# Latent attention's query columns: multiplied by pairs of heads, the rotated ones by fours

## The chip, the cores and the metric

One core of a Trainium2 chip runs the whole program: TensorE (PE) multiplies into PSUM banks, VectorE (DVE) and ScalarE (ACT) read these banks and write SBUF, GpSimd (POOL) works from SBUF to SBUF, SyncE (SP) issues the loads of weights. The metric is the device time of one launch in microseconds.

## The reference, cut to what matters

Two layers over 256 latent and 256 context tokens (512 in layer 0; in layer 1 queries are made for 256 tokens only). One of three branches of a layer is a latent attention with 8 heads. Its query vector has 64 plain and 32 rotated elements per head:

```
q = to_heads(rmsnorm(pq, lp['mla_q_norm_g']) @ lp['mla_w_uq'], MLA_HEADS)
q_nope, q_rope = q[..., :MLA_NOPE], q[..., MLA_NOPE:]
q_rope = apply_rope(q_rope, *rope)        # the 256 latent tokens only
q = jnp.concatenate([q_nope, q_rope], axis=-1)
s = jnp.einsum('bhqd,bhkd->bhqk', qi, k).astype(f32) * scale
```

`mla_w_uq` has 256 rows and 8 x 96 = 768 columns; head h owns columns 96h to 96h + 95, the last 32 of them rotated.

## The kernel before

Everything is float32 in effect: an operand is embedded in a float32r high part and a remainder (`split2`: ACT makes the high part, another engine subtracts), and `mm3` multiplies high by high, low by high and high by low, on lines 279, 280 and 281. A product over 256 rows is thus six multiplications.

`mla(l, nt)` has a stage ahead (projections, norms; `qn` the normed query input, `cn` the normed key/value input, both split) and a main stage. `split_uq` splits the query weights `raw` into `wqh` and `wql` in one piece of 128 x 1536. The main stage goes over four pairs of heads. `prod(p)` makes a pair's operands: one group of three multiplications for the keys of both heads, copied to `kh` and `kl`; then for each head six multiplications with 96 columns of weights into one PSUM bank of tag `g`; `rope` (L797 to L800) on rows 64 to 95 of that bank, four DVE operations on 32 x 256; and `split_scaled` (L803 on ACT, L804 on DVE) of all 96 rows into the head's tiles `qh` and `ql`. `A(h, u)` multiplies scores out of `qh`, `ql`, `kh`, `kl` into a bank of tag `s`: query blocks 0 and 1 against all 512 keys, in layer 0 also the context block. Maximum, exponential, transposes (`B`) and the product with the values (`C`) follow, two steps later.

Tag `g` has two banks. They serve keys, queries and also the convolution branch's and the gates' products that are woven in between. `qh` and `ql` have three tiles each. Temporaries come from a ring `t` of nine tiles (`t2k`). Steps are written as lists that are woven together and put in order by a table; each engine's instruction order then comes from the scheduler of the framework when the program is built, so that a change in one place moves neighbours on other engines. In layer 0 the multiplications of the modulation vectors (L347) stand between as work that waits for nothing here. POOL has only remainders (L219) and casts (L231) of weights, and a few convolution operations, in this stage.

`pick(key, default)` looks up which engine does a small copy.

Of the kernel before, what the change touches and what calls it, by code (L numbers as in the profile page):

```python
# [10 lines left out]
F32R = mybir.dt.float32r  # L11
# [7 lines left out]
D = 1024  # L19
# [3 lines left out]
MLA_SCALE = 96.0 ** -0.5  # L23
# [101 lines left out]
def backbone_kernel(ctx: ExitStack, tc: tile.TileContext, t, out):  # L125
# [3 lines left out]
    KDUP, WLO = "ee", (nc.vector, nc.vector)  # L129
# [5 lines left out]
    PE, ACT, DVE, POOL, SP = nc.tensor, nc.scalar, nc.vector, nc.gpsimd, nc.sync  # L135
# [25 lines left out]
    def t2k(dt=F32):  # L161
        return tmp.tile([128, 512], dt, tag="t", name="t")

    def bank(tag, bufs=2):
        return psum.tile([128, 512], F32, tag=tag, name=tag, bufs=bufs)
# [34 lines left out]
    def pick(key, default):  # L200
        return CHOICE.get(key, default)
# [4 lines left out]
    def cp(key, default="A"):  # L206

        return {"A": ACT.copy, "D": DVE.tensor_copy, "P": POOL.tensor_copy}[pick(key, default)]
# [66 lines left out]
    def mm3(ps, pairs, first=True, last=True):  # L275

        n = len(pairs)
        for i, (ah, al, bh, bl) in enumerate(pairs):
            PE.matmul(ps, lhsT=ah, rhs=bh, start=first and i == 0, stop=False)  # L279
            PE.matmul(ps, lhsT=ah, rhs=bl, start=False, stop=False)  # L280
            PE.matmul(ps, lhsT=al, rhs=bh, start=False, stop=last and i == n - 1)  # L281

    def split2(hi, lo, src, eng=DVE):

        ACT.copy(hi, src)
        eng.tensor_tensor(out=lo, in0=src, in1=hi.bitcast(F32), op=ALU.subtract)
# [506 lines left out]
    def rope(ps, rows, scr=True):  # L793

        a, b = t2k(), t2k()
        v = ps[rows, 0:NL]
        DVE.tensor_tensor(out=a[rows, 0:NL], in0=v, in1=rs[rows, :], op=ALU.mult)  # L797
        DVE.tensor_tensor(out=v, in0=v, in1=rc[rows, :], op=ALU.mult)
        DVE.stream_shuffle(out=b[rows, 0:NL], in_=a[rows, 0:NL], mask=SWAP16)
        DVE.tensor_tensor(out=v, in0=v, in1=b[rows, 0:NL], op=ALU.add)  # L800

    def split_scaled(hi, lo, src, scale):
        ACT.activation(out=hi, in_=src, func=AF.Copy, scale=scale)  # L803
        DVE.scalar_tensor_tensor(out=lo, in0=src, scalar=scale, in1=hi.bitcast(F32), op0=ALU.mult, op1=ALU.subtract)  # L804
# [58 lines left out]
    def mla(l, nt):  # L863

        pre, main = [], []
        box = {}
# [91 lines left out]

        def split_uq(raw, u):
            m = S["mla"]  # L960
            box["wq"] = (m.tile([128, 2, 768], F32R, name="wqh"), m.tile([128, 2, 768], F32R, name="wql"))
            split2(box["wq"][0], box["wq"][1], raw, WLO[l])

        bu = Blk(load_uq)
        bv = Blk(load_ukv)
        pre.append(Step(lambda u: None, Unit(bu, split_uq, late=True)))
        pre.append(Step(g_v, Unit(bv, split_ukv, late=True)))

        qt = {}

        def prod(p):
            def f():
                m = S["mla"]
                ps = bank("g")
                kc = slice(2 * p, 2 * p + 2)
                mm3(ps, [(box["wk"][0][:, kc, :].rearrange("p h d -> p (h d)"),
                          box["wk"][1][:, kc, :].rearrange("p h d -> p (h d)"), box["cn"][0], box["cn"][1])])
                for i in range(2):
                    kb = box["k"][(2 * p + i) % 3]
                    cp(f"kh{l}.{2 * p + i}")(kb[0][0:64, :], ps[64 * i:64 * i + 64, :])  # L980
                    DVE.tensor_tensor(out=kb[1][0:64, :], in0=ps[64 * i:64 * i + 64, :], in1=kb[0][0:64, :].bitcast(F32), op=ALU.subtract)
                for i in range(2):
                    h = 2 * p + i
                    ps = bank("g")
                    wc = slice(96 * h, 96 * h + 96)
                    mm3(ps[0:96, :nt], [(box["wq"][0][:, k, wc], box["wq"][1][:, k, wc],
                                         box["qn"][0][:, k, :], box["qn"][1][:, k, :]) for k in range(2)])
                    rope(ps, slice(64, 96))
                    qh = m.tile([128, nt], F32R, tag="qh", name="qh", bufs=3)
                    ql = m.tile([128, nt], F32R, tag="ql", name="ql", bufs=3)  # L990
                    split_scaled(qh[0:96, :], ql[0:96, :], ps[0:96, :nt], MLA_SCALE)
                    qt[h] = (qh, ql)
            return Step(f)

# [40 lines left out]
        for n in range(len(seq) + LAG + 2):  # L1035
            if n < len(seq):
                p, u, i = seq[n]
# [3 lines left out]
            if 0 <= n - LAG < len(seq):  # L1041
                p, u, i = seq[n - LAG]
# [641 lines left out]
```

## Time and profile before

| | us |
|---|---|
| three runs, median (lowest, highest) | 1326.32 (1324.16, 1326.61) |
| the profiled execution | 1327.46 |
| its span, first to last instruction | 1325.7 |
| PE busy | 1281.5 (97%) |
| DVE, ACT, POOL busy | 868.3 (66%), 579.7 (44%), 262.9 (20%) |

The span is what lies between the first and the last instruction; the execution's own time has 1.8 us more around it. Sums are made against that one execution. The two main stages that the change touches lie at about 97 to 195 us (layer 0) and 915 to 970 us (layer 1).

### The profile page before, as it was taken

How to read it: one execution, taken by the hardware profiler on the slowest of the kernel's cores; microseconds unless marked ns; L12 is line 12 of the kernel's file. 1: busy time of each engine (PE TensorE's matmuls, PEld its weight loads, DVE VectorE, ACT ScalarE, POOL GpSimd, SP SyncE). 2: the span in 40 equal slices, each digit the busy share in tenths (PEclk: the TensorE clock that was granted, in tenths of full speed). 3: DMA queues.
4: the chain of work that ended last, by engine and by line, in shares of the span. 5: the costliest groups of instructions: out<-in, count | busy, mean ns of one | idle time of the engine just before them, and what ended most of it. 6: DMA issues, size and time to landing. Idle time of an engine off the chain costs nothing. (4 is left out here: it accounts for less than half of the span.)

```text
span 1325.7 us, 19880 instructions
## 1 busy us (share of the span) xinstructions
PE 1281.5 (97%) x7934; PEld 1077.5 (81%) x7934; DVE 868.3 (66%) x1426; ACT 579.7 (44%) x1027; POOL 262.9 (20%) x233
## 2 busy tenths in 40 slices
PE   5999999999999999999999999998999999999997
PEld 3566777678888798787787877996788999999997
DVE  4776746865243568987584875588768557876555
ACT  4454552664222334332432331364546755645343
POOL 3111032210002112220100112122133343240210
PEclk8899999999999999999999999998999999999999
DMA  9643234443332324655563543332124355555552
GB/s 283 166 160 106 77 123 133 149 138 95 95 96 95 120 72 130 220 178 167 177 207 114 185 153 123 120 104 80 49 81 124 120 175 187 159 188 189 174 183 94
DMA packets 159790, 185.21 MB, mean 140 GB/s; under 512 B 4880, under 2 KB 149233, under 8 KB 157650
## 3 DMA queue, kind: packets, MB, share of 16 engines
q1 hardware_dynamic: 158162, 182.27, 43.7%
q0 software_dynamic: 928, 1.54, 0.4%
q8 instruction: 62, 1.02, 0.3%
q14 instruction: 30, 0.25, 0.1%
q10 hardware_dynamic: 608, 0.14, 0.0%
HBM read 182.88 MB, written 1.05 MB: 139 GB/s over the span
## 5 line engine op out<-in xcount | busy, mean ns | idle before, releaser
L231 ACT CAST whi<-raw 128x1024 fp32r<-128x1024 f32 x197 | 206.7, 1051 | 429.8 <-PE g L280 201.5
L279 PE MATMUL g<-hhi,whi 128*128 128x512 f32 (+2 forms) x1040 | 354.3, 341 | 4.3 <-DVE d L1179 1.7
L281 PE MATMUL g<-hhi,wlo 128*128 128x512 f32 (+2 forms) x1040 | 352.3, 339 | 0.1
L280 PE MATMUL g<-hlo,whi 128*128 128x512 f32 (+2 forms) x1040 | 351.9, 339 | 0.5 <-DVE hlo L506 0.5
L219 POOL TENSOR_TENSOR wlo<-raw,whi 128x512 fp32r<-128x512 f32 x138 | 187.6, 1380 | 647.3 <-ACT whi L231 508.2
L219 DVE TENSOR_TENSOR wlo<-raw,whi 128x1024 fp32r<-128x1024 f32 x161 | 199.7, 1242 | 151.0 <-ACT whi L231 144.5
L279 PEld LDWEIGHTS g<-hhi,whi 128*128 128x128 f32 x1040 | 195.4, 188 | 36.2 <-issue 4.7
L280 PEld LDWEIGHTS g<-hlo,whi 128*128 128x128 f32 x1040 | 196.1, 189 | 23.5 <-DVE hlo L506 0.7
L281 PEld LDWEIGHTS g<-hhi,wlo 128*128 128x128 f32 x1040 | 196.0, 189 | 22.7 <-issue 0.3
L383 DVE SCALAR_TENSOR_TENSOR macc<-modr,spad,macc 128x1024 f32<-128x1024 f32 x84 | 111.9, 1364 | 8.2 <-DMA modr<-in_w_mod_dram 7.5
L1364 DVE SCALAR_TENSOR_TENSOR x<-s,modT,x 128x256 f32<-128x256 f32 x95 | 43.5, 480 | 72.0 <-PE s L281 72.0
L281 PE MATMUL s<-hid0h,wlo 128*128 128x512 f32 (+1 forms) x256 | 86.9, 339 | 0.0
L280 PE MATMUL s<-hid0l,whi 128*128 128x512 f32 (+1 forms) x256 | 86.8, 339 | 0.0
L279 PE MATMUL s<-hid0h,whi 128*128 128x512 f32 (+1 forms) x256 | 86.7, 339 | 0.0
L279 PE MATMUL s<-hid1h,whi 128*128 128x256 f32 (+1 forms) x224 | 72.8, 325 | 0.0
L281 PE MATMUL s<-hid1h,wlo 128*128 128x256 f32 (+1 forms) x224 | 72.4, 323 | 0.0
L280 PE MATMUL s<-hid1l,whi 128*128 128x256 f32 (+1 forms) x224 | 72.4, 323 | 0.0
L809 DVE TENSOR_REDUCE sm<-s 128x1 f32<-128x512 f32 (+1 forms) x75 | 51.1, 689 | 30.2 <-PE s L281 17.3
L279 PEld LDWEIGHTS s<-hid0h,whi 128*128 128x128 f32 x256 | 48.4, 189 | 8.2 <-issue 1.7
L281 PEld LDWEIGHTS s<-hid0h,wlo 128*128 128x128 f32 x256 | 48.1, 188 | 5.7
L280 PEld LDWEIGHTS s<-hid0l,whi 128*128 128x128 f32 x256 | 48.0, 187 | 5.8
L157 ACT ACTIVATE t<-s,sm 128x512 f32<-128x512 f32 (+1 forms) x67 | 40.8, 614 | 26.0 <-DVE sm L809 25.7
(470 smaller groups left out, 2414.2 us busy)
## 6 DMA issues: line engine op xcount, KB each, us to landing
raw<-in_w_fc_dram SPq DMA_DIRECT2D x64, 1024.0 KB, 5.4
raw<-in_w_in_dram SPq DMA_DIRECT2D x34, 1024.0 KB, 5.3
modr<-in_w_mod_dram SPq DMA_DIRECT2D x48, 512.0 KB, 4.1
raw<-in_w_mod_dram SPq DMA_DIRECT2D x16, 1024.0 KB, 5.0
mq<-in_w_mod_dram SPq DMA_DIRECT2D x16, 512.0 KB, 7.7
raw<-in_w_out_dram SPq DMA_DIRECT2D x8, 1024.0 KB, 5.1
raw<-in_w_in_dram SPq DMA_DIRECT2D x8, 512.0 KB, 3.8
raw<-in_w_br_a_dram SPq DMA_DIRECT2D x8, 512.0 KB, 3.5
```

The lines of the kernel that those rows point to most:

```text
L157: ins = ACT.activation(out=out, in_=in_, func=func, **kw).ins
L219: e.tensor_tensor(out=u.lo[:, a:a + w], in0=src[:, a:a + w], in1=u.hi[:, a:a + w].bitcast(F32), op=ALU.subtract)
L231: cp(f"hi{u.id}")(u.hi, src)
L279: PE.matmul(ps, lhsT=ah, rhs=bh, start=first and i == 0, stop=False)
L280: PE.matmul(ps, lhsT=ah, rhs=bl, start=False, stop=False)
L281: PE.matmul(ps, lhsT=al, rhs=bh, start=False, stop=last and i == n - 1)
L383: DVE.scalar_tensor_tensor(out=a, in0=raw, scalar=sv, in1=a, op0=ALU.mult, op1=ALU.add)
L809: DVE.tensor_reduce(out=sm[:, c0:c0 + nseg], in_=ps.rearrange("p (s k) -> p s k", s=nseg), axis=AX.X, op=ALU.max, negate=True)
L1364: DVE.scalar_tensor_tensor(out=x[:, n, c], in0=ps[:, c], scalar=modT[l][:, goff + n, s:s + 1], in1=x[:, n, c], op0=ALU.mult, op1=ALU.add)
```

## The change

`split_uq` writes the columns in a new order: first the 64 plain columns of all heads (0 to 511), then the 32 rotated columns of all heads (512 to 767). It does so in four pieces (plain and rotated, for each of the two row halves). `prod(p)` multiplies the plain columns of both heads at once, 128 columns. In pairs 0 and 2 a further group multiplies the rotated columns of the next four heads, also 128; these are rotated together on 128 rows, scaled and split together into two tiles of the ring `t`, kept in `box["qr"]` for this pair and the next. Each head's `qh` and `ql` then get 64 rows from the pair's bank and 32 rows by a copy out of the common tiles, on POOL, since no key `qr...` is in the table of choices.

```diff
@@ -958,8 +958,13 @@
 
         def split_uq(raw, u):
             m = S["mla"]
+
             box["wq"] = (m.tile([128, 2, 768], F32R, name="wqh"), m.tile([128, 2, 768], F32R, name="wql"))
-            split2(box["wq"][0], box["wq"][1], raw, WLO[l])
+            for c0, d0, d in ((0, 0, 64), (512, 64, 32)):
+                hi, lo = [w[:, :, c0:c0 + 8 * d].rearrange("p k (h d) -> p k h d", d=d) for w in box["wq"]]
+                src = raw.rearrange("p k (h d) -> p k h d", d=96)[:, :, :, d0:d0 + d]
+                for k in range(2):
+                    split2(hi[:, k], lo[:, k], src[:, k], WLO[l])
 
         bu = Blk(load_uq)
         bv = Blk(load_ukv)
@@ -979,16 +984,27 @@
                     kb = box["k"][(2 * p + i) % 3]
                     cp(f"kh{l}.{2 * p + i}")(kb[0][0:64, :], ps[64 * i:64 * i + 64, :])
                     DVE.tensor_tensor(out=kb[1][0:64, :], in0=ps[64 * i:64 * i + 64, :], in1=kb[0][0:64, :].bitcast(F32), op=ALU.subtract)
+                def q_cols(c0):
+                    ps = bank("g")
+                    wc = slice(c0, c0 + 128)
+                    mm3(ps[:, :nt], [(box["wq"][0][:, k, wc], box["wq"][1][:, k, wc],
+                                      box["qn"][0][:, k, :], box["qn"][1][:, k, :]) for k in range(2)])
+                    return ps
+                if p % 2 == 0:
+                    ps = q_cols(512 + 64 * p)
+                    rope(ps, slice(0, 128))
+                    box["qr"] = (t2k(F32R)[:, :nt], t2k(F32R)[:, :nt])
+                    split_scaled(box["qr"][0], box["qr"][1], ps[:, :nt], MLA_SCALE)
+                ps = q_cols(128 * p)
                 for i in range(2):
                     h = 2 * p + i
-                    ps = bank("g")
-                    wc = slice(96 * h, 96 * h + 96)
-                    mm3(ps[0:96, :nt], [(box["wq"][0][:, k, wc], box["wq"][1][:, k, wc],
-                                         box["qn"][0][:, k, :], box["qn"][1][:, k, :]) for k in range(2)])
-                    rope(ps, slice(64, 96))
                     qh = m.tile([128, nt], F32R, tag="qh", name="qh", bufs=3)
                     ql = m.tile([128, nt], F32R, tag="ql", name="ql", bufs=3)
-                    split_scaled(qh[0:96, :], ql[0:96, :], ps[0:96, :nt], MLA_SCALE)
+                    split_scaled(qh[0:64, :], ql[0:64, :], ps[64 * i:64 * i + 64, :nt], MLA_SCALE)
+                    rows = slice(32 * (h % 4), 32 * (h % 4) + 32)
+                    for j, dst in enumerate((qh, ql)):
+                        e = pick(f"qr{l}.{h}.{j}", "P")
+                        {"P": POOL.tensor_copy, "D": DVE.tensor_copy, "A": ACT.copy}[e](dst[64:96, :], box["qr"][j][rows, :])
                     qt[h] = (qh, ql)
             return Step(f)
```

POOL in layer 0, from the weights' remainder ahead of pair 0 to the one after pair 1, before (`wlo` and `whi` are parts of weights, a number behind a name tells one tile from another):

```order
L483 TENSOR_TENSOR hlo_179<-t_433,hhi_178 128x256
L219 TENSOR_TENSOR wlo_863<-raw_850,whi_862 128x512 x2
L219 TENSOR_TENSOR wlo_1106<-raw_850,whi_1105 128x512 x2
L231 CAST whi_1546<-raw_1444 128x1024
L219 TENSOR_TENSOR wlo_1547<-raw_1444,whi_1546 128x512 x2
L219 TENSOR_TENSOR wlo_1552<-raw_1444,whi_1551 128x512 x2
```

and now, where `t_915` and `t_916` are the common high and low tile of heads 0 to 3:

```order
L219 TENSOR_TENSOR wlo_1099<-raw_856,whi_1098 128x512 x2
L1007 COPY qh_926<-t_915 32x512
L1007 COPY qh_932<-t_915 32x512
L1007 COPY ql_927<-t_916 32x512
L1007 COPY ql_933<-t_916 32x512
L1007 COPY qh_1038<-t_915 32x512
L1007 COPY ql_1039<-t_916 32x512
L231 CAST whi_1526<-raw_1439 128x1024
L219 TENSOR_TENSOR wlo_1527<-raw_1439,whi_1526 128x512 x2
L1007 COPY qh_1044<-t_915 32x512
L1007 COPY ql_1045<-t_916 32x512
L219 TENSOR_TENSOR wlo_1532<-raw_1439,whi_1531 128x512 x2
```

The copies stand in POOL's queue as high, high, low, low for heads 0 and 1; those of head 3 (`qh_1044`, `ql_1045`) have come behind a cast and a remainder.

TensorE in layer 0, pair 2, around the second group of query columns, before (`g_1252` is the bank of head 5, `s_1285` scores of head 4):

```order
L850 MATMUL o_1269<-t_1213,vtok_867 64x128
L347 MATMUL mod_1309<-raw_1544,spad_91 32x512 x3
L347 MATMUL mod_1309<-raw_1556,spad_91 32x512
L279 MATMUL s_1285<-kh1_772,qh_1248 128x512
L279 MATMUL g_1252<-qnh_706,wqh_846 96x512
L280 MATMUL g_1252<-qnl_707,wqh_846 96x512
L281 MATMUL g_1252<-qnh_706,wql_847 96x512
L279 MATMUL g_1252<-qnh_706,wqh_846 96x512
L280 MATMUL g_1252<-qnl_707,wqh_846 96x512
```

and now, where `g_1245` is the bank of the pair's plain columns (`t_1343` is a bank for transposes):

```order
L850 MATMUL o_1264<-t_1206,vtok_873 64x128
L347 MATMUL mod_1304<-raw_1524,spad_91 32x512 x2
L837 MATMUL t_1343<-ident_73,t_1215 128x128 x2
L279 MATMUL g_1245<-qnh_706,wqh_846 128x512
L280 MATMUL g_1245<-qnl_707,wqh_846 128x512
L281 MATMUL g_1245<-qnh_706,wql_847 128x512
L279 MATMUL g_1245<-qnh_706,wqh_846 128x512
L280 MATMUL g_1245<-qnl_707,wqh_846 128x512
L281 MATMUL g_1245<-qnh_706,wql_847 128x512
```

The scores of head 4 have gone behind the group, and two of the rows of L347 have gone from ahead of it.

ACT in layer 1, pair 2, before (`qh_7850` is head 4's tile, out of its own bank `g_7837`):

```order
L980 CAST kh1_7410<-g_7829 64x512
L157 ACTIVATE t_7825,ss_7739<-s_7821,sm_7826 128x512
L980 CAST kh2_7412<-g_7829 64x512
L803 ACTIVATE qh_7850<-g_7837 96x256
L840 COPY t_7876<-t_7871 128x512
L157 ACTIVATE t_7882,ss_7884<-s_7878,sm_7883 128x512
L803 ACTIVATE qh_7867<-g_7854 96x256
```

and now, where `g_7827` holds the plain columns of heads 4 and 5, and `t_7823` is the common high tile of heads 4 to 7:

```order
L985 CAST kh1_7390<-g_7802 64x512
L157 ACTIVATE t_7798,ss_7712<-s_7794,sm_7799 128x512
L985 CAST kh2_7392<-g_7802 64x512
L803 ACTIVATE qh_7834<-g_7827 64x256
L803 ACTIVATE t_7823<-g_7810 128x256
L840 COPY t_7851<-t_7846 128x512
L803 ACTIVATE qh_7840<-g_7827 64x256
L157 ACTIVATE t_7857,ss_7859<-s_7853,sm_7858 128x512
```

Head 4's plain rows are taken ahead of the common rotated tile, from a bank whose group comes later on TensorE.

## Rows read from the trace of the kernel before

**Rows 1.** Page, part 1: busy time, share of the span, instructions of each engine.

```profile
PE 1281.5 (97%) x7934; PEld 1077.5 (81%) x7934; DVE 868.3 (66%) x1426; ACT 579.7 (44%) x1027; POOL 262.9 (20%) x233
```

**Rows 2.** TensorE's waits, 205 to 1325 us: waiter, ender, sum, times, longest.

```profile
PE g L279 <- DVE x L1079: 2.6, 2, 2.5
...
PE g L279 <- ACT ge L1308: 0.2, 1, 0.2
```

**Rows 3.** Tile wqh, whole run: count, min/median/max ns, first and last start.

```profile
L279 PE MATMUL g<-qnh,wqh x32: 278/390/480, 97.6 to 954.3; 128*96 128x512 f32 x16, 128*96 128x256 f32 x16
...
L286 DVE TENSOR_TENSOR wql<-raw,wqh x2: 1748/1757/1766, 74.7 to 883.3; 128x1536 fp32r<-128x1536 f32 x2
```

**Rows 4.** Timeline, TensorE, layer 0, 512 tokens: start, length, line, tiles.

```profile
97.36 0.39 PE L281 MATMUL g<-cnh,wkl 128*128 128x512 f32 x1
97.59 0.39 PE L279 MATMUL g<-qnh,wqh 128*96 128x512 f32 x1
97.82 0.39 PE L280 MATMUL g<-qnl,wqh 128*96 128x512 f32 x1
```

**Rows 5.** Timeline, TensorE, layer 1, 256 tokens.

```profile
936.99 0.28 PE L279 MATMUL g<-qnh,wqh 128*96 128x256 f32 x1
937.11 0.28 PE L280 MATMUL g<-qnl,wqh 128*96 128x256 f32 x1
...
942.50 0.28 PE L279 MATMUL g<-hhi,whi 128*128 128x256 f32 x1
942.62 0.28 PE L280 MATMUL g<-hlo,whi 128*128 128x256 f32 x1
```

**Rows 6.** Line 1182 (copies of 32 rows), and timelines of POOL and DVE.

```profile
L1182 POOL CAST d<-d x21: 389/610/1629, 197.4 to 1017.0; 32x512 fp32r<-32x512 f32 x18, 32x256 fp32r<-32x256 f32 x3
...
1014.35 1.63 POOL L1182 CAST d<-d 32x512 fp32r<-32x512 f32 x1 [1.35 <-ACT d L1178]
...
1014.29 1.22 DVE L219 TENSOR_TENSOR wlo<-raw,whi 128x1024 fp32r<-128x1024 f32 x1
...
111.62 1.03 POOL L231 CAST whi<-raw 128x1024 fp32r<-128x1024 f32 x1 [16.42 <-PE s L281]
```

**Rows 7.** Timeline, layer 0, heads 0 and 1, DVE and TensorE.

```profile
102.38 0.69 DVE L804 SCALAR_TENSOR_TENSOR ql<-g,qh 96x512 fp32r<-96x512 f32 x1 [0.71 <-ACT qh L803]
...
103.95 0.39 PE L281 MATMUL s<-kh,ql 96*128 96x512 f32 x1
...
106.37 0.33 PE L837 MATMUL t<-ident,t 128*128 128x128 f32 x1 [0.33 <-ACT t L157]
106.85 0.50 PE L279 MATMUL s<-kh,qh 96*128 96x512 f32 x1 [0.15 <-ACT qh L803]
```

**Rows 8.** Timeline, layer 0, pair 2, TensorE and DVE.

```profile
137.97 1.07 PE L347 MATMUL mod<-raw,spad 128*32 128x512 f32 x8
...
139.31 0.40 PE L279 MATMUL g<-qnh,wqh 128*96 128x512 f32 x1
...
138.39 0.69 DVE L804 SCALAR_TENSOR_TENSOR ql<-g,qh 96x512 fp32r<-96x512 f32 x1
```

**Rows 9.** Layer 1: a window's busy times and granted clock, then timeline rows.

```profile
core 0: us, PE busy (x) PEld busy (x) DVE busy (x) ACT busy (x) POOL busy (x), PEclk, DMA share, GB/s
917.00:924.00 7.00, 5.66 (x17) 4.25 (x16) 5.57 (x15) 1.65 (x5) 0.00 (x0) 0.51 0.00 0
...
918.92 0.80 PE L279 MATMUL s<-kh,qh 96*128 96x512 f32 x1 [1.34 <-ACT qh L803]
...
920.37 0.63 PE L279 MATMUL g<-cnh,wkh 128*128 128x512 f32 x1
920.80 0.63 PE L280 MATMUL g<-cnl,wkh 128*128 128x512 f32 x1
...
940.16 0.33 PE L279 MATMUL g<-qnh,wqh 128*96 128x256 f32 x1 [0.25 <-DVE kl L981]
...
941.70 0.50 PE L279 MATMUL s<-kh,qh 96*128 96x512 f32 x1 [0.61 <-ACT qh L803]
...
941.26 0.38 ACT L803 ACTIVATE qh<-g 96x256 fp32r<-96x256 f32 x1 [2.16 <-DVE g L800]
```

## The prediction

> **What bounds the kernel now.** I read the page's first part, then TensorE's waits, then the two stages that the change touches as a timeline. The first row to see is that TensorE is busy for 97% of the span [rows 1]. That alone says little, since a busy engine may still be waiting for its next operand, so the second view is what ended its idle time after 205 us: the list has 19 rows, the largest is 2.6 us, the smallest 0.2, every one names a compute engine and none a DMA [rows 2]. Two things follow. A multiplication that is no longer there shortens the run by its distance from the next one, wherever TensorE's queue is dense. And time won early is kept: no transfer is waited for later that would take it back.
>
> **The multiplications.** One head's query columns are six multiplications with 96 columns of weights; in both layers together that is 32 on each of the three lines, so 96 [rows 3]. After the change one pair takes six with 128 columns, and every second pair six more for the rotated columns of four heads: per layer (4 + 2) x 6 = 36 in place of 48. The price of one is the distance to the next start. With 512 tokens (layer 0) it is 0.23 us behind 128 columns of weights and 0.23 behind 96 [rows 4]; with 256 tokens (layer 1) 0.12 behind either [rows 5]. So the wider weights cost nothing and the 24 that go are worth 12 x 0.23 + 12 x 0.12 = 4.2 us. All of them go in the odd pairs: pair 1 and pair 3 have six where they had twelve, while pairs 0 and 2 keep twelve.
>
> **What the change adds to the way from the multiplication to the scores.** Before: rotation on DVE, scaled copy on ACT, remainder on DVE, then the scores. Now a head's scores also need its 32 rotated rows copied by POOL from the common tile, one copy for the high part and one for the low. Such copies are in the trace elsewhere: 0.61 us for 512 columns, 0.39 for 256, once 1.63 [rows 6]. I follow the four places where the queues could not hide them.
>
> Layer 0, pair 0. The first scores start as before, since the rotation group stands where head 0's group stood. The remainder of that group ended at 102.38 + 0.69 = 103.07 and the scores' third multiplication, which reads it, began at 103.95 [rows 7]. In POOL's new order two high copies are in front of the low one, but they need only ACT's part and run while DVE makes the remainder; the low copy begins at about 103.6 and ends at 104.2. That is 0.25 us late, and the new order of TensorE puts one key multiplication ahead of it: between 0 and 0.25, taken 0.15. On the other side head 1 no longer has a rotation of its own: the idle of 0.33 at 106.37 and of 0.15 at 106.85 [rows 7] closes, and with it one slower first multiplication, 0.6 together. Bounds of this place: -0.75 to +0.5 (if copies in a row leave gaps), taken -0.45.
>
> Layer 0, pair 2. The pair's group needs the bank that the rotation group holds until DVE has taken the remainder. Before, the second group began at 139.31, and from 137.97 on eight modulation multiplications (1.07 us) and one of the scores stood in front of it [rows 8]. In the new order half of the eight stand there and the one of the scores comes later, so on the old scale TensorE would be there at 137.97 + 0.5 = 138.5, while DVE's remainder ends at 138.39 + 0.69 = 139.1. So 0.6 us are laid bare, 0.7 with a slower first multiplication; none if DVE, with fewer operations, comes that much earlier. Taken 0.7, ends 0 and 1.5.
>
> Layer 1, pair 0. Here everything waits already: TensorE runs at half clock from 917 to 924, granted 0.51 [rows 9]. The copies replace the second rotation that DVE put between; taken +0.15, ends 0 and 0.6.
>
> Layer 1, pair 2. Scores began at 941.70, 0.44 after ACT began its scaled copy of 0.38, at 941.26, with 0.61 us idle [rows 9]. Now ACT takes head 4's plain rows first; these wait for the pair's group, which begins at 940.16; its last of six starts 0.64 later and takes 0.28 [rows 5]. So about 941.1, plus 0.38 for these, 0.38 for the rotated tile, 0.4 for POOL's copy: 942.3. That is 0.6 more, and the low copy comes fourth in POOL's queue (0.39 each), 0.25 more after what TensorE has to fill with. Taken +0.85, ends 0.4 and 1.5. Before pair 3 DVE makes no rotation any more, so a wait like the 0.25 us at 940.16 (for a key remainder that stands behind a rotation [rows 9]) goes there: -0.2.
>
> **Off the path.** The rotation: eight times four operations become two times four per layer, on four times the rows; DVE gets time back, but where TensorE waits for it is counted above, so nothing more. The weights' split was one remainder of 1.76 us [rows 3]; in four pieces, each at most as long as the remainder of 0.69 in [rows 8], it is 2.8 at most. It lies at 74.7 and 883.3 us, over twenty us ahead of its use; nothing. In layer 1 the scheduler places some of its surroundings anew, among conv operations that TensorE waits for (up to 2.6 us by [rows 2]); I see neither sign, 0 with ends -0.7 and +0.7. The transfers of the transform tables, which POOL issues behind the copies, are wanted only after the stage.
>
> **The sum**, against the profiled execution: -4.2 (multiplications) - 0.45 + 0.7 (layer 0) + 0.15 + 0.85 - 0.2 (layer 1) = -3.15 us. Its time is 1327.46 us (span 1325.7, 1.8 around it), so 1324.3; the median of the runs shown, 1326.32, lies 1.1 below that execution, so as a median I say 1323.2. With every place at its upper end (0.5, 1.5, 0.6, 1.5, and 0.7 ahead of layer 1's stage) nothing is left, +0.4; with every one at its lower end (-0.75, 0, 0, 0.4, -0.7) it is -5.5.
>
> **Rivals.**
> *The chains eat it.* POOL's copies are behind one another and, in layer 0, head 3's two stand behind a cast and a remainder of weights. That cast began at 111.62 after a wait of 16.42 us for TensorE [rows 6]; cast, remainder and copies are done some 5 us later, at 117, and head 3's scores come at about 119. If the places come out half way to their upper ends, 1.8 of the 3.15 goes: 1325.0. For it: all four are chains over three engines, which I read from one execution. Against: the idle in the trace where such chains stand is small.
> *The clock.* The low stretch from 917 costs 0.20 us for each multiplication of 512 columns (distance 0.43 in [rows 9] against 0.23), eleven of them, and 0.10 for two of 256: 2.4. It came after idle of 2.5 [rows 2] and 1.34 us [rows 9] on TensorE. If the shorter rotation of pair 0 (one in place of two on DVE) or other work there keeps the clock up: 1323.2 - 2.4 = 1320.8. If instead the idle at layer 1's pair 2 (0.25 and 0.61 before, some 1.5 then) brings a second such stretch: 1325.6.
> *Copies at the long price (the slower side).* One copy of the 21 took 1.63 us in place of 0.61; it began at 1014.35, beside a DVE subtraction of 1.22 at 1014.29 whose two inputs both lie in SBUF [rows 6]. If the copies here met the same, each on the path would cost 1.0 in layer 0 and 0.65 in layer 1; three and two of them stand in a row in front of scores in layer 0 (pairs 0 and 2), five and four in layer 1: 5 x 1.0 + 9 x 0.65 = 10.9 us, so 1323.2 + 10.9 = 1334. It decides from six long copies on: these eat the 3.15 and 2.65 more. Against it: beside the copies DVE mostly has one input in PSUM here (rotation, remainders, maxima); its subtractions of two SBUF tiles come once per pair, for the outputs.
> This is where a rule speaks against the change. The Trainium skill, "SBUF — State Buffer", section "Who interferes with whom", says: "A DVE instruction with two SBUF inputs contends with a GpSimd instruction that reads SBUF", and that the first to issue holds the shared port for its whole length. The copy of 1.63 us agrees with it; by that rule taken for every copy the time is the 1334 above, and by the row of 0.61, which the other copies show, it is the forecast.
> *It does not do what it says* would be 24 multiplications still there; the order of the new program excludes it.
>
> **How the numbers follow.** A measurement of this kernel tells about 0.2% from no change, so 2.65 us, and the forecast lies just beyond. Chances: forecast 0.52 (1321.8 to 1324.8; 0.34 of it past 2.65, 0.18 short of it); the clock kept up or layer 1's start better placed 0.12, faster; the chains 0.22, within 0.2%; a second low stretch 0.04, within; long copies or a queue that POOL blocks 0.10, slower. Faster 0.46, same 0.44, slower 0.10. The range takes in all but the last and the outermost ends: 1319.8 to 1327.0.
>
> **What would show it.** In the new profile TensorE must have 24 multiplications fewer, still 0.23 and 0.12 apart. At 104 us the scores' low part comes some 0.2 later, and the idle at 106.4 is gone. At about 137 us idle of 0.5 to 0.9 ends with DVE's remainder of the rotated tile. At about 940 us the idle in front of the scores is over 1 us and ends with POOL. The copies take 0.61 and 0.39. If pair 1 of layer 0 doesn't end two microseconds earlier than before, the first step is wrong; if the clock is low elsewhere than near 917 to 924, or copies of over 1 us stand in front of scores, a rival holds; if DMA waits appear on TensorE after 205 us, the claim that time is kept is wrong.

## The result: slower, 1.0064 of the time before

| | us |
|---|---|
| before, median of 4 runs beside the changed kernel's (lowest, highest) | 1326.46 (1324.16, 1326.81) |
| after, median of 4 runs (lowest, highest) | 1334.12 (1331.61, 1337.11) |
| ratio of after to before, 95% interval | 1.0064 (1.0050 to 1.0078) |
| profiled execution of after, its span | 1331.61, 1329.6 |

The prediction was 1323.2 within 1319.8 to 1327.0. The measured time is 10.9 above the forecast and 7.1 above the range. The first part of the page of after answers to [rows 1]:

```profile
PE 1281.5 (96%) x7910; PEld 1077.3 (81%) x7910; DVE 850.9 (64%) x1376; ACT 582.6 (44%) x1037; POOL 279.8 (21%) x265
```

TensorE has the promised 24 instructions fewer, and yet it is busy just as long: 1281.5 us. Fewer instructions and no less busy time means that something else on TensorE became dearer. The pitch did not: behind 128 columns of weights it is 0.23 us in layer 0 and 0.12 in layer 1, as said. The timeline of after, TensorE, one stretch of each layer (start, length, line, tiles):

```profile
95.70 0.40 PE L279 MATMUL g<-qnh,wqh 128*128 128x512 f32 x1
95.94 0.39 PE L280 MATMUL g<-qnl,wqh 128*128 128x512 f32 x1
...
939.79 0.28 PE L280 MATMUL g<-qnl,wqh 128*128 128x256 f32 x1
939.90 0.28 PE L281 MATMUL g<-qnh,wql 128*128 128x256 f32 x1
```

### Where the time went

To find the place I matched each multiplication of the two traces by its line, tiles and shape, in order, and took the start in after less the start in before. Up to 72 us the two programs have the same instructions in the same order on every engine, and yet after is 1.9 us earlier at 70 to 90 us: that is chance of the two executions (in the traces of all versions the lag at 70 us lies between -2.24 and +3.72). What counts is how this number, the lag, moves from there:

| stretch, on before's scale (us) | lag at its start | at its end | expected movement | measured |
|---|---|---|---|---|
| 90 to 190: layer 0's main stage | -1.86 | -2.32 | -2.5 | -0.46 |
| 200 to 205: behind it | -2.32 | -0.42 | 0 | +1.90 |
| 205 to 885: the rest of layer 0 | -0.42 | -0.76 | 0 | -0.34 |
| 885 to 910: layer 1's pre stage | -0.76 | +2.48 | 0 | +3.24 |
| 910 to 985: layer 1's main stage | +2.48 | +2.42 | -0.64 | -0.06 |
| 985 to the end | +2.42 | +3.91 | 0 | +1.49 |

(Of the sum, -2.5 is 12 x 0.23 with -0.45 and +0.7; -0.64 is 12 x 0.12 with +0.15, +0.85 and -0.2.) Three rows of this table are wrong by 1.9 us or more. Each has a mark in the trace.

**The modulation multiplications (L347).** In layer 0's main stage they are work that waits for nothing. Both kernels run 56 of them between 96 and 195 us, before in 9 groups, after in 11. The timeline of after, TensorE, with the row behind each group:

```profile
103.92 1.07 PE L347 MATMUL mod<-raw,spad 128*32 128x512 f32 x8
104.91 0.50 PE L281 MATMUL s<-kh,ql 96*128 96x512 f32 x1
...
165.67 1.05 PE L347 MATMUL mod<-raw,spad 128*32 128x512 f32 x4
166.66 1.09 PE L857 MATMUL o<-t,vtok 128*64 128x128 f32 x16
167.68 1.04 PE L347 MATMUL mod<-raw,spad 128*32 128x512 f32 x2
168.66 0.39 PE L279 MATMUL s<-kh,qh 96*128 96x256 f32 x1
```

From the start of a group to the next instruction it is 0.99 us for eight, 0.99 for four and 0.98 for two. A group has one price, whatever its size up to eight, where nothing behind it waits. Summed over the 56, the distances are 10.13 us before and 11.72 after. In these, 1.06 and 0.80 are idle in front of the next instruction; without it, 9.07 and 10.92, so the two groups more cost 1.85. All of TensorE's distances between 92 and 193 us, by kind: query columns -3.1, idle -0.4, modulation +1.85, scores and products with the values, whose order moved too, +1.0, the rest +0.15, together the -0.46 of the table. (The Trainium skill, "TensorEngine Tiling (Array Packing)", section "Key Properties", says that changing the tiling mode drains TensorE; a price per group agrees with that, but no run here takes the drain apart from the rest.) The prediction saw the eight of [rows 8] split in two and charged only the wait that this lays bare.

**A load that comes too late, layer 0.** These groups also read a buffer. Weights come through a ring of two raw buffers, loaded by SP's queue in order; a load waits until the last reader of its buffer is done. The timelines of SP, before and then after (L340 loads modulation weights, L263 the projection weights that the next stage needs):

```profile
113.27 26.15 SPq L340 DMA_DIRECT2D raw<-in_w_mod_dram  x3
...
174.67 9.67 SPq L263 DMA_DIRECT2D raw<-in_w_in_dram  x2
```

```profile
110.88 56.21 SPq L340 DMA_DIRECT2D raw<-in_w_mod_dram  x3
...
179.90 9.26 SPq L263 DMA_DIRECT2D raw<-in_w_in_dram  x2
```

The first row's three loads have all gone out by 139.4 before (113.27 + 26.15), and only by 167.1 after (110.88 + 56.21). SP's waits in after, 95 to 225 us, name the reader (waiter, ender, sum, times, longest):

```profile
SPq L340 <- PE mod L347: 64.6, 6, 39.4
```

39.4 us in one wait: it ends with the group of 165.67, whose load before was read by the eight of 137.97 [rows 8]. All later loads move with it: the last L263 has gone out by 189.2 in place of 184.3. It takes some 5 us, then ACT casts it, and TensorE waits behind ACT. ACT's cast, before and then after, and TensorE's wait in after; before, there is no wait on TensorE between 196 and 215 us:

```profile
193.93 1.05 ACT L242 CAST whi<-raw 128x1024 fp32r<-128x1024 f32 x1 [4.49 <-PE g L280]
```

```profile
194.03 1.05 ACT L242 CAST whi<-raw 128x1024 fp32r<-128x1024 f32 x1 [6.75 <-DMA raw<-in_w_in_dram]
...
201.99 0.44 PE L357 MATMUL t<-ident,t 128*128 128x128 f32 x2 [1.64 <-ACT ut L1130]
```

Against the work around it, which comes 2.3 earlier in after, the load is 4.9 + 2.3 = 7.2 us late. Before, by the same 5 us, it was there 4.6 us ahead of its cast (184.3 + 5 against 193.93; an estimate), so some 2.6 are laid bare, of which TensorE sees 1.9.

**A load that comes too late, layer 1.** SP's waits between 872 and 890 us, before and then after:

```profile
SPq L263 <- DVE wql L286: 9.6, 1, 9.6
...
SPq L933 <- POOL wlo L219: 2.6, 1, 2.6
```

```profile
SPq L263 <- POOL wlo L219: 2.8, 1, 2.8
...
SPq L933 <- DVE u L1093: 0.6, 1, 0.6
```

Before, the projection load L263 took the buffer that the query weights' split (`wql`) had read, and the load L933 the one that POOL had read. After, they have changed places: L263 waits for POOL's `wlo`, L933 goes out right behind it. The order of the loads is the same; the buffers are exchanged. The timelines of SP, before and after:

```profile
885.15 0.37 SPq L263 DMA_DIRECT2D raw<-in_w_in_dram  x1
888.69 0.34 SPq L933 DMA_DIRECT2D raw<-in_mla_w_ukv_dram  x1
```

```profile
888.69 0.37 SPq L263 DMA_DIRECT2D raw<-in_w_in_dram  x1
889.16 0.52 SPq L933 DMA_DIRECT2D raw<-in_mla_w_ukv_dram  x1
```

Against the work around it, which comes 0.8 earlier in after, the load is 3.5 + 0.8 = 4.3 us late. The exchange is not all of this. DVE's last piece of the split ends later too, since other work of DVE now stands between the pieces. DVE, before and then after:

```profile
883.32 1.77 DVE L286 TENSOR_TENSOR wql<-raw,wqh 128x1536 fp32r<-128x1536 f32 x1
```

```profile
886.87 0.66 DVE L286 TENSOR_TENSOR wql<-raw,wqh 128x256 fp32r<-128x256 f32 x1
```

The query weights' buffer was free at 885.09 before and is free at 887.53 after. Without the exchange the load would still have been 2.4 + 0.8 = 3.2 us late; the exchange adds 1.1. No run takes the two apart.

The chain of waits of after runs through just this load (start, length, what), and ends on TensorE, whose own row stands last:

```profile
885.94 2.73 POOL wlo L219 x2
888.69 5.34 DMA raw<-in_w_in_dram
...
894.12 0.69 DVE whi L231
...
902.33 0.57 ACT t L1090
```

```profile
903.02 0.35 PE L279 MATMUL g<-hhi,whi 128*128 128x256 f32 x1 [3.58 <-ACT t L1090]
```

TensorE had been idle for 3.58 us, and half clock followed, where before it ran at full clock. The window of 904 to 908 us, after and then before (length, busy PE, PEld, DVE, ACT and POOL, granted clock, DMA):

```profile
904.00:908.00 4.00, 4.00 (x21) 3.83 (x19) 2.63 (x5) 0.37 (x1) 2.73 (x4) 0.57 0.87 257
```

```profile
904.00:908.00 4.00, 2.63 (x14) 1.81 (x13) 3.99 (x8) 1.72 (x3) 0.88 (x2) 1.00 0.50 130
```

**The copies.** Their waits are in the trace, within the ends foretold. TensorE in after, in front of the scores of pairs 0 and 2 of layer 1, and all 16 high copies of the run (count, min/median/max ns):

```profile
922.39 0.50 PE L279 MATMUL s<-kh,qh 96*128 96x512 f32 x1 [1.46 <-POOL qh L1007]
...
923.75 0.50 PE L281 MATMUL s<-kh,ql 96*128 96x512 f32 x1 [0.39 <-POOL ql L1007]
...
944.95 0.50 PE L279 MATMUL s<-kh,qh 96*128 96x512 f32 x1 [1.26 <-POOL qh L1007]
...
L1007 POOL CAST qh<-t x16: 389/500/609, 100.6 to 954.5; 32x512 fp32r<-32x512 f32 x8, 32x256 fp32r<-32x256 f32 x8
```

1.46 stands against 1.34 before, 1.26 against 0.61 [rows 9]; the waits of 0.39 and, at pair 2, of 0.16 for the low copies are new.

### The profile page after: what moved, and what is told of

Same layout as the page of the kernel before. It is cut to its first block, busy times and chain, and to the rows that moved or that the text cites. A ratio compares the mean times of both kernels' runs of the same rounds, so it can differ in the third digit from the quotient of the medians.

```text
span 1329.6 us, 19868 instructions
## 1 busy us (share of the span) xinstructions
PE 1281.5 (96%) x7910; PEld 1077.3 (81%) x7910; DVE 850.9 (64%) x1376; ACT 582.6 (44%) x1037; POOL 279.8 (21%) x265
## 3 DMA queue, kind: packets, MB, share of 16 engines
HBM read 182.88 MB, written 1.05 MB: 138 GB/s over the span
## 4 chain that ended last, share of the span: by engine, by line
PE 79%; DVE 9%; DMA 4%; ACT 4%; issue 2%; POOL 1%; ACTq 0%; SPq 0%; DVEq 0%; POOLq 0%
PE g L279 14%; PE g L280 14%; PE g L281 14%; PE s L279 9%; PE s L281 9%; PE s L280 9%; PE o L850 2%; PE t L837 2%; ACT whi L231 1%; DMA raw<-in_w_in_dram 1%; PE mod L347 1%; DVE wlo L219 1%; DMA raw<-in_w_fc_dram 1%; POOL wlo L219 1%; DMA raw<-in_w_out_dram 1%
```

## The experiments

The theory after these readings, W: two loads come late, one because the split in four pieces exchanges two buffers (layer 1), one because modulation groups stand later (layer 0), and the copies cost about what was said. The main rival, C: the chain over POOL's copies (or the half clock that its waits bring) costs the time, and the loads are late without anyone waiting. The times are medians; each ratio is to the kernel before on the same chip.

**The split alone.** The kernel before, with its query columns in their old order, but split in four pieces. No pairs, no copies.

```diff
-            split2(box["wq"][0], box["wq"][1], raw, WLO[l])
+            for d0, d in ((0, 64), (64, 32)):
+                hi, lo, src = [w.rearrange("p k (h d) -> p k h d", d=96)[:, :, :, d0:d0 + d] for w in (*box["wq"], raw)]
+                for k in range(2):
+                    split2(hi[:, k], lo[:, k], src[:, k], WLO[l])
```

> The kernel before, with one edit: the query weights are split in the same four pieces as in the changed kernel (their columns stay where they were), and nothing else is changed: no pairs, no copies. Theory W (weight loads): in layer 1 the load that took the query weights' buffer as soon as their remainder was done (885.15 us before) now takes another buffer and waits for POOL's remainder, so it is issued at about 888.7, the weights' cast behind it comes at about 894, and the stage ahead of the attention loses 4 to 6 us: 1330 to 1332. Rival C (the chains over POOL's copies cost the time): no copies here, so the time of the kernel before, 1326.3, within 1 us.

Measured: 1329.89, ratio 1.0022 (1.0011 to 1.0034), 0.1 below the range of W. The edit, which the prediction priced at nothing, makes the kernel before 3.4 us slower by itself. SP's waits and TensorE's timeline of this kernel show the same exchange:

```profile
SPq L263 <- POOL wlo L219: 2.8, 1, 2.8
...
906.56 0.55 PE L279 MATMUL g<-hhi,whi 128*128 128x256 f32 x1 [3.60 <-ACT t L1077]
```

Its lag rises by 3.0 across layer 1's pre stage (+2.76 to +5.80), and rises nowhere else. W holds in kind, with no copy in the program at all. (The last piece of the split ends late here too, at 891.04, and the load goes out at 892.20.)

**The split in two pieces.** The changed kernel, plain and rotated columns each split for both row halves at once.

```diff
-                for k in range(2):
-                    split2(hi[:, k], lo[:, k], src[:, k], WLO[l])
+                split2(hi, lo, src, WLO[l])
```

> The changed kernel, with its weight split in two pieces (plain and rotated columns, both row halves at once) in place of four; pairs, fours and copies as they are. In the built order the loads take the same buffers as in the kernel before. Theory W: the load is issued at about 885 again and the 4 to 6 us in front of layer 1's attention come back: 1327.5 to 1330 against 1334 of the changed kernel. Rival C: the copies are all there, so 1333 to 1335.

Measured: 1329.96, ratio 1.0030 (1.0017 to 1.0042), 4.2 below the changed kernel. SP's timeline has the two loads apart again, as in the kernel before:

```profile
887.71 0.37 SPq L263 DMA_DIRECT2D raw<-in_w_in_dram  x1
890.87 0.34 SPq L933 DMA_DIRECT2D raw<-in_mla_w_ukv_dram  x1
```

Layer 1's lag now moves by 0.2 (+2.18 to +2.38), though the waits for POOL's copies are all there (the longest 1.78). So the loss of layer 1 is the load, not the copies. Layer 0 still loses as before: its late load and an idle of 1.74 us remain.

**One layer at a time.** The whole change in layer 0 only, and in layer 1 only; the other layer keeps the old code.

```diff
+        split_uq = split_uq_new if l == 0 else split_uq_old
+        prod = prod_new if l == 0 else prod_old
```

> The change in layer 0 alone, layer 1 as before. Theory W: the 12 multiplications' 2.8 us are given back in layer 0 (the modulation's multiplications stand in more and smaller groups, and one of their weight buffers comes free 27 us later, so a later weight load is late and TensorE waits 1.6 us at 202): +0.5 to +2 us against before, 1327 to 1328.5. Rival C, by which only chains like those of layer 1 at 922 and 945 us cost: layer 0 keeps its gain, 1323.5 to 1324.5.

> The change in layer 1 alone, layer 0 as before. Theory W: the exchanged buffer is there (load at about 888.7), so most of the loss: +4 to +7 us, 1330.5 to 1333.5. Rival C: the copies' two chains, 1.5 us of idle each where 1.3 and 0.6 stood before, less 1.4 for the multiplications: 1326 to 1327.5.

Measured: layer 0 alone 1328.49, ratio 1.0010 (0.9998 to 1.0022); layer 1 alone 1331.56, ratio 1.0042 (1.0026 to 1.0057). Neither is a gain. Together they make +2.0 and +5.1, so 7.1 of the 7.7 of the changed kernel: the two losses add up, as far as intervals of some 1.6 and 2.1 us to either side can tell.

**The modulation step earlier.** The two-piece kernel with one modulation step put earlier in the list of steps (place 72 to place 60), so that its buffer is read early.

```diff
+    for i, j in ((72, 60),):
+        prog.insert(j, prog.pop(i))
```

> The changed kernel with the split in two pieces, and one step of the modulation (the one whose four multiplications stood 2 and 2, at 134 and 166 us, in the changed kernel) written 12 steps earlier in the list of steps, so that the scheduler puts its four multiplications together again at the second pair. Theory W: its weight buffer is free at about 134 us again, the loads behind it in SyncE's queue go out 5 to 25 us earlier, TensorE's wait of 1.7 us at 204 goes, and the modulation stands in as many groups as in the kernel before: layer 0 gains 2 to 2.5 us against before, layer 1 is about even: 1323.8 to 1325.5. Rival (the copies or the pairs themselves hold layer 0 back, the order of the modulation does not): as with two pieces alone, 1329 to 1330.5.

Measured: 1329.64, ratio 1.0020 (1.0010 to 1.0031). That is a miss, no better than without the move, and the trace says why. The stage itself now gained 4.2 us up to 193 us (eight groups, 8.91 us), but the *next* modulation step had moved nowhere, its group ran at 170.8, and it held the ring's other buffer. SP's timeline, TensorE's waits after 195 us, and a window:

```profile
171.86 0.38 SPq L263 DMA_DIRECT2D raw<-in_w_in_dram  x1
...
181.39 10.23 SPq L263 DMA_DIRECT2D raw<-in_w_in_dram  x2
...
PE t L357 <- ACT ut L1129: 3.6, 1, 3.6
...
204.00:208.00 4.00, 3.45 (x18) 3.31 (x19) 3.01 (x8) 2.16 (x4) 0.81 (x2) 0.66 0.34 141
```

The last load has gone out by 191.6, TensorE stands idle for 3.6 us, and half clock follows. The lag goes from -1.68 to +3.64: all of the gain and 1.1 more is given back. Freeing one buffer of two is not enough.

**The copies on ACT and DVE.** The two-piece kernel with the high copies on ACT and the low ones on DVE.

```diff
-                        e = pick(f"qr{l}.{h}.{j}", "P")
+                        e = "AD"[j]
```

> The changed kernel with the split in two pieces, and the rotated rows copied by ACT (high part) and DVE (low part) in place of POOL; the modulation is left where the scheduler puts it (one of its two late buffers comes free early again, the other late). Theory W: POOL's copies are a small part: layer 1's two waits on POOL of 1.8 and 1.3 us become waits on ACT or DVE of about 1 each, and half of layer 0's loss goes: 1 to 3 us below the kernel with two pieces, 1327 to 1329. Rival C (POOL's copies cost most of it): 1324 or less.

Measured: 1327.99, ratio 1.0010 (0.9998 to 1.0022), 2.0 better than with POOL. But the wait before pair 0's scores of layer 1 is not shorter: 1.63 us on ACT's copy, where POOL's took 1.78. What became better: in layer 1 the waits for the copies sum to 2.8 us against 3.4 with POOL, and the lag falls by 1.4 (+3.10 to +1.73) where it rose by 0.2. Layer 0's stage gained 2.3 by 193 us (+0.29 to -1.97) against 0.45 with POOL, with nine modulation groups in place of eleven; behind it, 4.65 were lost to a late load again (-1.97 to +2.68).

**Both together.** Two pieces, the copies on ACT and DVE, and the modulation step at place 60.

> Both: split in two pieces, the modulation's step written 12 steps earlier, copies on ACT and DVE. Theory W: the gain in layer 0 of 2 to 2.5 us and about 0.5 to 1 in layer 1: 1323 to 1325. Rival C: no better than the kernel with the copies on ACT and DVE alone.

Measured: 1323.83, ratio 0.9977 (0.9967 to 0.9987). This is the only version here that is clearly faster than the kernel before, by 2.6 us. The edit moved one modulation step, as in the run that missed; here the scheduler took the second along, and the two ran as one group of fourteen, so both buffers came free early. That was luck: no expectation had it. TensorE's and SP's timelines:

```profile
135.82 1.92 PE L347 MATMUL mod<-raw,spad 128*32 128x512 f32 x14
...
137.79 0.38 SPq L263 DMA_DIRECT2D raw<-in_w_in_dram  x1
...
174.26 8.22 SPq L263 DMA_DIRECT2D raw<-in_w_in_dram  x2
```

The last load has gone out by 182.5 (before: 184.3), and TensorE has no wait between 195 and 215 us. Layer 0's stage gains 2.53 us (lag -0.15 to -2.68), and this time it is kept. That it equals the 2.5 of the prediction's sum is chance: the sum is for copies on POOL and has other terms in it.

**The rotated group a pair earlier.** The same kernel, with the rotated columns of heads 4 to 7 multiplied at the end of pair 1's products, so that pair 2 doesn't wait for them.

```diff
-                if p % 2 == 0:
+                def rot(p):
                     ps = q_cols(512 + 64 * p)
...
+                if p == 0:
+                    rot(0)
...
+                if p == 1:
+                    rot(2)
```

> As the one before, and the rotated group of heads 4 to 7 multiplied, rotated and split one pair earlier, so that pair 2's scores do not wait for it. Theory W: the wait in front of pair 2's scores in layer 1 (1.3 us in the changed kernel) shrinks to 0.6 or less, and layer 0's pair 2 has no wait for the bank: 0.5 to 1 us less than without it, 1322.5 to 1324.5. Rival: the two tiles of the ring held for a pair longer hold up the softmax, 1325 or more.

Measured: 1327.69, ratio 1.0015 (1.0001 to 1.0029), a miss. The wait that it aims at is gone (one wait for `qh` is left in place of two), but the scheduler placed the second modulation group at 173.9 again: the last load had gone out by 194.6 only, with 3.48 us idle on TensorE behind it. An edit in the attention had moved a load once more, as the change itself does. The profiled execution, 1333.39, is the slowest of the twelve, so its trace shows where time goes and not how much of it is in the median.

**Are the two causes the whole loss?** If so, mending both in the changed kernel must bring it back to the time before, with POOL's copies in place. The first of the next two runs mends only layer 0 (two modulation steps earlier, four pieces), the second both.

```diff
+    for i, j in ((72, 60), (78, 68)):
+        prog.insert(j, prog.pop(i))
```

> The changed kernel as it is (four pieces, POOL's copies), with two steps of the modulation written earlier, so that their buffers come free at the second and third pair as in the kernel before. Theory W: the last weight load ahead of the differential branch (188.8 us in the changed kernel, 184.0 before) goes out at 185 or earlier, TensorE's wait of 1.6 us at 202 goes, layer 1 keeps its loss: 2.5 to 4 us less than the changed kernel's 1334, 1330 to 1332. Rival: layer 0's loss is in the pairs and copies themselves: 1333.5 to 1335.

> The same with the split in two pieces, so with both late loads mended and all copies on POOL. Theory W: 1324.5 to 1326.5, at or a little below the kernel before; what is then left to the kernel with copies on ACT and DVE (1323.8) is the price of POOL's copies, 0.5 to 2.5 us. Rival C (POOL's copies cost most of the loss): 1328 or more.

Measured: 1329.64, ratio 1.0022 (1.0013 to 1.0031), 0.4 below its range, and 1325.68, ratio 0.9999 (0.9989 to 1.0008). With the changed kernel and the two-piece one these make a square:

| median, us | modulation as it came | two steps earlier |
|---|---|---|
| split in four pieces | 1334.12 | 1329.64 |
| split in two pieces | 1329.96 | 1325.68 |

Each cause has its price in either line and column: 4.5 and 4.3 for the modulation, 4.2 and 4.0 for the pieces (the kernel before ran at 1326.5 beside the left column and at 1326.2 beside the right one). The price of the modulation holds two things that these runs do not separate, the load that is in time and one group fewer (ten in place of eleven). The two causes add up, and without them the change is worth nothing measurable: 0.5 below the kernel before in these medians, within its interval, and not the 3.15 that the prediction's sum had. In the trace of the last run layer 0's stage gains 1.75 (lag +0.91 to -0.84) and layer 1 0.5 (-0.85 to -1.31). In the first of the two the exchange is still there in layer 1, in the second the loads of layer 0 are in time. SP's timelines of the one and the other:

```profile
886.11 0.37 SPq L263 DMA_DIRECT2D raw<-in_w_in_dram  x1
886.58 0.52 SPq L933 DMA_DIRECT2D raw<-in_mla_w_ukv_dram  x1
```

```profile
176.09 8.17 SPq L263 DMA_DIRECT2D raw<-in_w_in_dram  x2
```

**A late load put into the kernel before.** The old code, with one modulation step later (place 78 to 90). Nothing of the change is in it.

```diff
+    for i, j in ((78, 90),):
+        prog.insert(j, prog.pop(i))
```

> The kernel before, with nothing but one step of the modulation written 12 steps later: three of its four multiplications move behind the first transforms, and its weight buffer is held until then. No pairs, no copies. Theory W: the loads behind it in SyncE's queue are late, TensorE waits at about 195 to 210 us where it waited for nothing: 2 to 6 us more, 1328.5 to 1332.5. Rival (no wait of TensorE on a transfer after 205 us in the trace of before, so a later load costs nothing): 1325.5 to 1327.

Measured: 1331.25, ratio 1.0036 (1.0026 to 1.0046), 5.1 slower. Loads of SP, and TensorE's waits after 195 us:

```profile
186.37 7.80 SPq L263 DMA_DIRECT2D raw<-in_w_in_dram  x2
...
PE t L357 <- ACT ut L1114: 1.8, 1, 1.8
```

The last load has gone out by 194.2, ten us later than before, and the same wait for `ut` appears that the changed kernel has. So the place does not need the change to lose time; it needs only a late reader of a raw buffer.

**The early group again, with three steps moved.** The version with the rotated group a pair earlier, and modulation steps put earlier so that no load is late.

```diff
+    for i, j in ((66, 59), (72, 61), (78, 63)):
+        prog.insert(j, prog.pop(i))
```

> Copies on ACT and DVE, split in two pieces, the rotated group of heads 4 to 7 one pair earlier, and three steps of the modulation written earlier. Theory W: loads in time, and pair 2 of layer 1 without the wait of 1.2 us: 1322.5 to 1324.5. Rival: the modulation in more groups and the tiles held longer take it back: 1325 to 1327.

Measured: 1327.34, ratio 1.0006 (0.9992 to 1.0019), the second miss with this edit. The wait behind the stage is gone, but the stage itself loses 4.7 us (lag -0.52 to +4.22): a new idle of 2.38 us ends with ACT, and half clock up to 178.4 costs some 2.7 more, estimated from the distances of these rows against those at full clock. Why ACT is late there no run tells apart. TensorE's timeline and a window:

```profile
172.40 1.97 PE L857 MATMUL o<-t,vtok 128*64 128x128 f32 x14 [2.38 <-ACT t L840]
...
172.00:176.00 4.00, 3.60 (x21) 3.05 (x22) 1.92 (x4) 2.91 (x7) 1.77 (x2) 0.50 0.32 76
```

In layer 1 one wait for `qh` is left (1.7 us), and the lag falls by 3.4 (+4.28 to +0.90). That is more than the wait that the edit removes: the granted clock is 1.00 in every window from 896 to 952 us here, where before had 0.51 from 917 to 924 [rows 9].

## Why the prediction was wrong

**Right.** The 24 multiplications and their pitch: in layer 0 the query columns' distances are 2.9 to 3.1 us shorter in all versions that keep the change there, against 2.8 in the sum. The copies: 0.61 and 0.39 us, never more than 0.612 in all 32, so the rival of copies at the long price is false; that its 1334 is the measured time is chance. The Trainium skill, "SBUF — State Buffer", section "Who interferes with whom", whose rule was weighed there, is not contradicted by this: the runs here have no copy of the long kind, and the DVE instructions with two inputs beside the copies of after all read one of them from a PSUM bank (`g`). The idle at 106.4 closed. Layer 1's waits for POOL came where they were said: +0.12 and 0.39 at pair 0 (0.51, taken 0.15, ends 0 and 0.6), +0.65 and 0.16 at pair 2 (0.81, taken 0.85).

**Wrong, the split ("it lies over twenty us ahead of its use; nothing").** I asked who waits for the split's *output*. What mattered was its *input*: the raw buffer, which the next load takes. With one piece, that load took the buffer that the split frees, and went out at 885.15; with four pieces the split freed its buffer 2.4 us later, and the framework gave the load the other, freed by POOL, so that it went out at 888.69. Why it chooses so, no run shows. Price 3.0 us in the trace and 3.4 in the median of the split alone, with 4.0 to 4.2 in the square.

**Wrong, "time won early is kept: no transfer is waited for later".** The list of waits has no DMA in it after 205 us [rows 2], and in after it still has none on TensorE: the waits end with ACT and DVE, `ut` and `t`. But ACT's cast of 194.03 waited 6.75 us for a DMA, and in layer 1 DVE's at 894.12 waited 1.13. Apart from the modulation groups TensorE reads no raw weights itself, so a late load must show as a wait for ACT or DVE. "No DMA in TensorE's waits" was true and proved nothing. The margin of 4.6 us in front of the cast of 193.93 was the number to read, and the queue ahead of that load.

**Wrong, layer 0's pair 2 (+0.7).** The foretold idle of 0.5 to 0.9 us did not come; other products stood in the place. In its stead two more groups cost 1.85, other orders of scores and value products 1.0, and the group that was put off to 165.67 held a buffer and cost 1.9 more behind the stage. The order had shown the eight in two halves; I priced the hole that they left and not the second start, nor the load queued behind their buffer.

**Not foreseen, layer 1's pair 1.** The wait for a key remainder before pair 3 went as foretold (0.19 us at 953.87 before, none after). But a new one of 0.60 us stands at pair 1, for which the sum has no term. With pair 0's 0.51 in place of 0.15 it is as much as layer 1's main stage lacks and more: -0.06 in place of -0.64. TensorE's timeline of after:

```profile
930.55 0.36 PE L279 MATMUL g<-hhi,whi 128*128 128x256 f32 x1 [0.60 <-DVE kl L986]
```

**The clock.** The second low stretch was a rival, at the wrong place: it came at 904 us, behind the idle of 3.58, not at pair 2. From 885 to 910 us the loss of 3.24 divides into 2.13 us more idle (the 3.58 and a wait of 1.05, less waits that before has there) and 1.11 of multiplications farther apart. The idle of 1.34 us that the prediction put ahead of the low stretch of before lies inside it: the row at 917.17, ahead of that idle, takes 0.41 us where those up to 916.91 take 0.28.

**Open.** From 985 us on after loses 1.5 us more. Four waits of the output stage there are longer by 0.2 to 0.3 each (1.1 together), all on DVE and ACT work that the change doesn't touch; with the modulation earlier this end moves by 0.4, and with two pieces besides by -0.2, so I don't know whether it belongs to the kernel or to that execution. From 970 us on all engines have the same instructions in the same order in all versions, and this end moves by anything from -1.7 (the split alone) to +1.5 (after): that speaks for the execution. The medians also differ by 7.7 us where the two profiled executions differ by 4.2. Of the 3.5 between, 1.9 is the start of after's execution up to 72 us; for the rest, after's four runs lie between 1331.61 and 1337.11, and no trace shows what the slower ones wait for. All lags are against one execution of before, 1327.46, which is 1.0 to 1.3 us above its medians. Nor do the runs fully say why the copies on ACT and DVE are 1.9 us better than on POOL (1323.83 against 1325.68, both with the loads in time). In layer 1 the waits before the scores sum to 2.5 us against 3.6, and its lag falls by 2.8 against 0.5; but the modulation groups and the low clock stretches stand differently in the two, and the trace of the former is the fastest of twelve executions.

## What to carry to other kernels

When an edit changes how often or when a staging buffer is read, ask when the last reader is done, which load takes that buffer next, and follow it to its use; with a ring of two, both buffers must come free in time. Don't read "no DMA among TensorE's waits" as "no load is late": look at the casts that read what is loaded, and at how little they wait. And work that waits for nothing is not free to move: each further group has a price of its own, and so has what it holds while it is put off.

## What the runs showed of the hardware

A group of modulation multiplications (32 columns of weights, 512 columns) at full clock takes 0.98 us for two, 0.99 for four, 0.99 for six, 1.00 for eight and 1.85 for fourteen, from its start to the next instruction, where that does not wait. Half clock (a granted 0.50 to 0.66 in windows of the profile, multiplications of 256 columns 0.21 apart in place of 0.12) stood behind each idle of 3.2 to 3.6 us that TensorE had in these runs, seven in all, and behind the one of 2.38. Behind the idles of 1.64 to 1.85 at 202 to 204 us there was none: behind the 1.64 at 201.99, in the window of 204 to 208, the clock was 1.00. Every trace has an idle of 2.46 us ahead of layer 1's pair 0, at 913 to 923 us. In ten of the fourteen, half clock stands at its end or soon behind it; in three it came only behind the next wait, of 1.78 us; in the early group's second run there was none. In layer 0, where before waits for nothing, such an idle cost more than its length: 5.3 us in all for an idle of 3.56, 4.7 for 3.23 and 6.2 for 3.48. In layer 1 the 3.58 cost 3.24, since waits that before has there were gone.
